# The first nine slots of an RWKV "wkv" kernel: set-up work, a state chain, zero matmuls and load order rearranged

## The chip, the cores and the metric

The kernel runs on one core of one Trainium2 chip. The metric is the device time of one execution in microseconds. A profiled execution also has a span, from its first instruction to its last, and the granted clock of TensorE.

## The reference

The inputs are k and v of 16 batches x 2048 steps x 256 channels in float32, and two rows w and u of 256. For each batch and channel a recurrence runs over time, kept in a scaled form (aa, bb, with the exponent pp):

```
for t in range(seq_len):
    kk, vv = k[b, t, :], v[b, t, :]
    ww = u + kk
    qq = max(pp, ww);  e1 = exp(pp - qq);  e2 = exp(ww - qq)
    output[b, t, :] = (e1 * aa + e2 * vv) / (e1 * bb + e2 + 1e-08)
    ww = pp - w + kk
    qq = max(ww, kk);  e1 = exp(ww - qq);  e2 = exp(kk - qq)
    aa = e1 * aa + e2 * vv;  bb = e1 * bb + e2;  pp = qq
```

So an output is a weighted mean of all earlier v, with weights that decay with w, plus the present one with its bonus u.

## The kernel before, in words

Time is cut into a head of T0 = 32 steps and 16 pieces ("steps" c = 0 to 15) of TC = 126, each of two halves of 63. A pair is one step with 4 of the 16 batches: time on the partitions, 4 x 256 channels along the free axis as two chunks of 512. Two pairs more (n = 2 and 3) hold the head for all batches. That makes 66 pairs; step 0 has the pairs 0, 1, 4 and 5.

The main loop (lines 636 to 693) has one slot n for each pair and 12 more. Its order is the order of the instructions on each engine, since the helper K pins every instruction behind the one issued before it on the same engine. In slot n:

- load(n + 6) issues the next loads; from pair 6 on k and v are both issued on POOL (lines 122 and 144). Each of k and v has six buffers. The first six k are issued on SP, the first v on POOL.
- exps(n) (ScalarE, lines 337 and 339) takes the exponential of X, two sets of logarithmic weights in PSUM, into the bf16 tile ez. Before pair 8 X is two tiles of two banks, each with an activation of its own; from pair 8 on it is one tile of four banks and one activation of 2048 columns, taken from a new pool (line 315).
- round_k(n + 1) (VectorE, line 307) copies the next k to float32r, and logs(n + 1) (TensorE, line 323) multiplies it by the matrices NLE and NLZ: four matmuls into X.
- times_v(n) (VectorE, line 346) multiplies half of ez by v; sums(n) (TensorE, line 377) adds rows of ez for the state.
- for a pair finished earlier: den (TensorE, line 525) and log_den (ScalarE, line 534) for q, invert (ScalarE, line 539) one slot later, and num (TensorE, line 547), mult (VectorE, line 555) and store two slots later. q is n - 10, for the head n - 6. So the head pairs have their den in slots 8 and 9, and pair 0 has it in slot 10.

Between steps a state is carried. The table PLANS places each part of it, as (slots after the last pair of the step, place in the slot, function): "a" places lie in ScalarE's order, "d" in VectorE's, "p" in TensorE's. small_work(n, place) issues what stands there. Within a slot the places come in the order a3, exps, d0, round_k, p0, num, d1, a0, p1, invert, a2, den and log_den, mult, d2, d3, a4, logs, num, p3, times_v and sums, p2, d4, mult and store, d5, p4, a1. For step 0 (plan "first", last pair 5) the parts are: copy_sums (ScalarE), turn_sums (TensorE), split_sums (VectorE, gives tsum), state_logs (ScalarE, gives lf), state_offset and state_near (VectorE), state_weights (ScalarE, w and g), state_sums, state_add and state_decay (VectorE, AB), inject_logs and inject_weights (ScalarE, y and phi), carry_weights and carries (VectorE, phi2 and ab), turn_carries (TensorE), and inject (line 495): VectorE copies the turned carries to row, and SP issues four DMAs of 8 KB that write them into rows 126 and 127 of the ez tiles of this step. den reads these two rows: for pair 0 the first two of the four DMAs must have landed. The plan "head" is a shorter chain for the pairs 2 and 3.

PSUM has eight banks: X four, psd (tag "den") two, psn (tag "num") one, pst (the sums) one. Until slot 66 den, turn_sums and turn_carries share the one psd tile, so each waits until the reader of the one before is done; psn holds the sums of the head until copy_sums, and num from slot 10 on.

Ahead of the loop stand the constant matrices. TensorE begins with 12 matmuls of zeros into psn (line 216). matrices_for_head (VectorE) stands at slot 0, place d1; the matrices that den and num need, matrices_for_outputs (It, Id, IdN), matrices_for_outputs_of_head (Lh, LhN) and more_matrices_for_outputs (Lf, LfN), stand at place d5 of slots 3, 4 and 5 (lines 627 to 629).

Of the kernel before, what the change touches and what calls it, by code (L numbers as in the profile page):

```python
# [7 lines left out]
F32 = mybir.dt.float32  # L8
# [14 lines left out]
def kernel(  # L23
# [32 lines left out]
    D = 2 * Dm  # L56
# [3 lines left out]
    AHEAD = 6  # L60
# [50 lines left out]
    def load(n):  # L111
        kr = kpool.tile([128, 4, Dm], F32, tag="kr", name="kr")
        vr = vpool.tile([128, 4, Dm], BF16, tag="vr", name="vr")
        kr_of[n], vr_of[n] = kr, vr
        c, p = pairs[n]
        if is_head(n):
            load_head(n, SP, kr, k)
        else:
            t0 = T0 + c * TC
            r = min(128, T - t0)  # L120

            K((SP if n < AHEAD else POOL).dma_start(  # L122
                out=kr[0:r, :, :], in_=k[4 * p:4 * p + 4, t0:t0 + r, :].rearrange("n t d -> t n d")))
            if n >= AHEAD:
                load_v(n)

    def load_head(n, eng, t, x):
# [25 lines left out]
    def row_of(a, b):  # L153
        return crow[a:b, :].unsqueeze(1).broadcast_to([b - a, 4, Dm])

    for n in range(AHEAD):
        load(n)
    K(SC.preload_act_table_set("natural_log_exp_and_others"))

# [49 lines left out]
        K(DVE.tensor_scalar(E[:, 0:N], E[:, 0:N], cw, None, ALU.add))  # L209


    zeros = consts.tile([128, D], BF16, tag="zeros", name="zeros")
    fill(zeros, 0.0)
    idle = psn.tile([128, D], F32, tag="num", name="idle")
    for i in range(12):
        K(PE.matmul(idle, zeros[:, 0:128], zeros, start=True, stop=True))

    for x in (kr_of, vr_of):
        fill(x[3][64:96, 0:2, :], 0.0)
# [371 lines left out]
    PLANS = {  # L591
        "head": ((1, "a0", copy_sums), (1, "p2", turn_sums), (2, "d1", split_sums), (2, "a1", state_logs),
                 (3, "a0", state_weights), (3, "d4", state_start)),
        "first": ((1, "a0", copy_sums), (1, "p3", turn_sums), (1, "d5", split_sums), (1, "a1", state_logs),
                  (2, "d1", state_offset, 0), (2, "d1", state_offset, 1), (2, "d1", state_near),
                  (2, "a0", state_weights), (2, "d3", state_sums), (2, "d3", state_add, 0),
                  (2, "d3", state_decay, 0), (2, "a1", inject_logs), (2, "a1", inject_weights),
                  (3, "d0", carry_weights), (3, "d0", carries), (3, "p0", turn_carries), (3, "d1", inject),
                  (3, "d4", state_add, 1), (3, "d5", state_decay, 1)),
        "steady": ((1, "a0", copy_sums), (1, "p2", turn_sums), (2, "d1", split_sums), (2, "a2", state_logs),  # L600
                   (2, "d3", state_offset, 0), (2, "d4", state_offset, 1), (2, "d5", state_near),
                   (3, "a0", state_weights), (3, "d2", state_sums), (3, "d3", state_add, 0),
# [33 lines left out]
    for n in range(NP + LAG + 2):  # L636
# [90 lines left out]
```

## Time and profile before

| what | value |
|---|---|
| median of 4 runs | 297.68 us (296.36 to 299.38) |
| the profiled execution | 298.33 us |
| its span | 296.6 us |
| its mean granted TensorE clock | 0.942 of full |
| ACT (ScalarE) busy | 264.9 us, 298 instructions |
| DVE (VectorE) busy | 252.9 us, 520 instructions |
| PE (TensorE) busy | 252.3 us, 1144 matmuls |
| POOL (GpSimd) busy | 162.1 us, most of it issuing DMAs |
| ACT busy in the first 45 us | 30.3 us |

All times of the trace are in microseconds from the start of the span. PEld is TensorE's weight load, which runs beside its matmuls; a name with q behind it (SPq) is the engine's sequencer, which issues DMAs. A line of a timeline gives start, length, engine, line of the kernel, operation, what it writes and reads (out<-in) with shapes, and in brackets the idle time of the engine ahead of it and what ended that. The row of digits gives the busy share, or the granted clock, of 40 equal slices in tenths.

### The profile page before, as it was taken

How to read it: one execution, taken by the hardware profiler on the slowest of the kernel's cores; microseconds unless marked ns; L12 is line 12 of the kernel's file. 1: busy time of each engine (PE TensorE's matmuls, PEld its weight loads, DVE VectorE, ACT ScalarE, POOL GpSimd, SP SyncE). 2: the span in 40 equal slices, each digit the busy share in tenths (PEclk: the TensorE clock that was granted, in tenths of full speed). 3: DMA queues.
4: the chain of work that ended last, by engine and by line, in shares of the span. 5: the costliest groups of instructions: out<-in, count | busy, mean ns of one | idle time of the engine just before them, and what ended most of it. 6: DMA issues, size and time to landing. Idle time of an engine off the chain costs nothing.

```text
span 296.6 us, 3976 instructions
## 1 busy us (share of the span) xinstructions
PE 252.3 (85%) x1144; PEld 115.8 (39%) x1144; DVE 252.9 (85%) x520; ACT 264.9 (89%) x298; POOL 162.1 (55%) x227
## 2 busy tenths in 40 slices
PE   8598688788999989889989898998989898788970
PEld 3245343344434434443434343444434443333430
DVE  5767668979998989999999999998999999778760
ACT  7665679789999999999999999999999999798990
POOL 8786346755665665565666555567655652212531
PEclk9855579999999999999999999999999999999995
DMA  6999999999999999999999999999999999245885
GB/s 184 249 275 303 302 254 203 257 293 290 296 322 333 333 330 332 330 335 342 333 331 327 330 324 329 337 342 336 320 335 321 325 311 271 89 146 189 281 269 183
DMA packets 59253, 85.94 MB, mean 290 GB/s; under 512 B 6834, under 2 KB 43430, under 8 KB 59232
## 3 DMA queue, kind: packets, MB, share of 16 engines
q0 software_dynamic: 52608, 81.73, 100.6%
q1 hardware_dynamic: 6592, 3.94, 5.0%
q8 instruction: 9, 0.15, 0.2%
q14 instruction: 12, 0.10, 0.1%
q10 hardware_dynamic: 32, 0.02, 0.0%
HBM read 68.12 MB, written 34.05 MB: 344 GB/s over the span
## 4 chain that ended last, share of the span: by engine, by line
ACT 29%; DVE 23%; PE 21%; issue 14%; DMA 11%; SPq 0%; POOL 0%; ACTq 0%; DVEq 0%; POOLq 0%
ACT ez L339 12%; ACT rd L534 8%; PE X L323 8%; DVE rd L555 7%; DVE ez L346 7%; ACT rd L539 5%; PE num L547 5%; PE den L525 4%; DMA kr<-in_k_dram 4%; DMA vr<-in_v_dram 4%; DVE km L307 3%; DMA out_dram<-rd 3%; PE tot L377 2%; PE den L395 2%; DVE ts L388 1%
## 5 line engine op out<-in xcount | busy, mean ns | idle before, releaser
L339 ACT ACTIVATE ez<-X 128x2048 bf16<-128x2048 f32 x58 | 109.3, 1885 | 6.1 <-PE num L547 3.9
L555 DVE TENSOR_TENSOR rd<-num,rd 128x512 f32<-128x512 f32 (+2 forms) x131 | 88.7, 685 | 8.6 <-ACT rd L539 4.3
L144 POOL DMA_DIRECT2D vr<-in_v_dram x64 | 54.7, 854 | 74.1 <-DVE ez L346 21.7
L346 DVE TENSOR_TENSOR ez<-ez,vr 126x2048 bf16<-126x2048 bf16 (+1 forms) x66 | 79.9, 1210 | 7.1 <-ACT ez L339 4.0
L575 POOL DMA_DIRECT2D out_dram<-rd x63 | 51.5, 818 | 48.8 <-issue 18.5
L534 ACT ACTIVATE rd<-den 128x1024 f32<-128x1024 f32 (+3 forms) x67 | 67.3, 1005 | 4.0 <-PE den L525 3.5
L539 ACT ACTIVATE rd<-rd 128x1024 f32<-128x1024 f32 (+3 forms) x67 | 70.3, 1049 | 0.3
L547 PE MATMUL num<-ez,LfN 128*128 128x512 bf16 x128 | 49.1, 384 | 10.0 <-DVE rd L555 9.9
L323 PE MATMUL X<-km,NLE 128*128 128x512 f32 x128 | 51.2, 483 | 7.4 <-ACT ez L339 2.5
L547 PE MATMUL num<-ez,IdN 126*128 126x512 bf16 (+1 forms) x131 | 49.8, 380 | 0.0
L307 DVE CAST km<-kr 126x1024 fp32r<-126x1024 f32 x64 | 47.8, 747 | 2.2 <-DMA kr<-in_k_dram 2.2
L122 POOL DMA_DIRECT2D kr<-in_k_dram x60 | 46.5, 774 | 2.9 <-issue 2.3
L323 PE MATMUL X<-km,NLZ 128*128 128x512 f32 x128 | 42.9, 418 | 0.0
L525 PE MATMUL den<-ez,Id 126*128 126x512 bf16 (+1 forms) x131 | 39.6, 382 | 0.0
L525 PE MATMUL den<-ez,Lf 128*128 128x512 bf16 x128 | 38.0, 378 | 1.8 <-DVE tsum L402 0.7
L323 PEld LDWEIGHTS X<-km,NLE 128*128 128x128 f32 x128 | 21.8, 200 | 25.6 <-ACT ez L339 14.7
L377 PE MATMUL tot<-ez,OHV 126*32 126x512 bf16 x128 | 26.5, 406 | 4.8 <-DVE ez L346 4.7
L323 PEld LDWEIGHTS X<-km,NLZ 128*128 128x128 f32 x128 | 25.7, 201 | 6.4 <-ACT ez L337 0.4
L377 PE MATMUL tot<-ez,OHE 128*32 128x512 bf16 x128 | 26.5, 411 | 0.0
L547 PEld LDWEIGHTS <-LfN 128*128 128x128 bf16 x128 | 12.3, 96 | 23.1 <-issue 20.5
L525 PEld LDWEIGHTS <-Lf 128*128 128x128 bf16 x128 | 12.4, 98 | 20.5 <-issue 8.6
L337 ACT ACTIVATE ez<-X 128x1024 bf16<-128x1024 f32 (+1 forms) x16 | 14.6, 966 | 5.6 <-PE X L323 5.5
(108 smaller groups left out, 195.9 us busy)
## 6 DMA issues: line engine op xcount, KB each, us to landing
out_dram<-rd POOLq DMA_DIRECT2D x60, 512.0 KB, 7.3
kr<-in_k_dram POOLq DMA_DIRECT2D x56, 512.0 KB, 8.3
vr<-in_v_dram POOLq DMA_DIRECT2D x60, 256.0 KB, 7.5
kr<-in_k_dram SPq DMA_DIRECT2D x4, 512.0 KB, 9.1
kr<-in_k_dram POOLq DMA_DIRECT2D x4, 504.0 KB, 8.8
ez<-row SPq DMA_DIRECT2D x64, 8.0 KB, 5.6
vr<-in_v_dram POOLq DMA_DIRECT2D x4, 252.0 KB, 8.1
out_dram<-rd POOLq DMA_DIRECT2D x2, 504.0 KB, 4.4
```

Source lines behind the costliest of these rows:

```text
L144: K(POOL.dma_start(out=vr_of[n][0:r, :, :], in_=v[4 * p:4 * p + 4, t0:t0 + r, :].rearrange("n t d -> t n d")))
L307: K(DVE.tensor_copy(KM[n][0:r, 0:i, :], kr_of.pop(n)[0:r, 0:i, :]))
L323: K(PE.matmul(X[q][:, i, :], m[0:kr, :], km[0:kr, i, :], start=True, stop=True))
L339: K(SC.activation(ez_of(n)[:, 0:4:2], X[2][:, :, 0:i, :], ACT.Exp))
L346: K(DVE.tensor_mul(ez[0:r, 1:4:2], ez[0:r, 0:4:2], vb[0:r].unsqueeze(1).broadcast_to([r, 2, i, D])))
L377: K(PE.matmul(TOT[c][y:y + 32], m[0:r, :], ez_of(n)[0:r, q, i, :], start=n == first_of[c], stop=n == last_of[c] or (head and i == 1), tile ...
L525: K(PE.matmul(d[:, i, :], m[0:r, :], ez_of(n)[0:r, q, i, :], start=q == 0, stop=q == 2, skip_group_check=True))
L534: K(SC.activation(RD[n][0:r, a:b, :], DEN[n][0:r, a:b, :], ACT.Ln, scale=RS))
L539: K(SC.activation(RD[n][0:r, a:b, :], RD[n][0:r, a:b, :], ACT.Exp, scale=-1.0))
L547: K(PE.matmul(d, m[0:r, :], ez_of(n)[0:r, q, i, :], start=q == 1, stop=q == 3, skip_group_check=True))
L555: K(DVE.tensor_mul(RD[n][0:r, i, :], NUM.pop((n, i))[0:r, :], RD[n][0:r, i, :]))
L575: K(eng.dma_start(out=out[4 * p + a:4 * p + b, t0:t0 + r, :].rearrange("n t d -> t n d"), in_=o[0:r, a:b, :]))
```

## The change

It makes five edits, all of them to the first nine slots.

1. Loads. k of pairs 0 and 1, and of the head, stay on SP; k of pairs 4 and 5 move from SP to POOL and are issued behind the v loads of pairs 2 and 3, each followed by its own v.
2. The 12 zero matmuls at the start write to psd instead of psn. In every slot from 0 to 8 two more follow logs(n + 1), and two more follow sums(n) (not in slot 4). Slots up to 4 (up to 3 behind the sums) use psd, the later ones psn.
3. The plan "head": state_logs moves from the end of slot 5 (a1) to slot 6, place a0, behind its exps.
4. The plan "first": state_logs moves from the end of slot 6 to slot 7, a0, behind the exps; state_offset and state_near from d1 to d3 of slot 7; state_weights to slot 8, a3, ahead of its exps; state_sums, state_add and state_decay to slot 8, d0; inject_logs and inject_weights to slot 8, a0, behind its exps; carry_weights and carries from d0 to d3 of slot 8; turn_carries from p0 to p3; inject from d1 to d4; state_add and state_decay of the second half to slot 9, d2 and d4.
5. The matrices for the outputs move to place d2 of slots 0, 1 and 2.

```
@@ load
-            K((SP if n < AHEAD else POOL).dma_start(
+            K((SP if n < 2 else POOL).dma_start(
                 out=kr[0:r, :, :], in_=k[4 * p:4 * p + 4, t0:t0 + r, :].rearrange("n t d -> t n d")))
-            if n >= AHEAD:
+            if n >= 2:
                 load_v(n)
...
-    for n in range(AHEAD):
+    for n in range(4):
         load(n)
...
-    idle = psn.tile([128, D], F32, tag="num", name="idle")
-    for i in range(12):
-        K(PE.matmul(idle, zeros[:, 0:128], zeros, start=True, stop=True))
+
+    def idle(pool, count):
+        t = pool.tile([128, D], F32, tag="num", name="idle") if pool is psn else pool.tile(
+            [128, 2, D], F32, tag="den", name="idle")[:, 0]
+        for i in range(count):
+            K(PE.matmul(t, zeros[:, 0:128], zeros, start=True, stop=True))
+
+    idle(psd, 12)
...
-    for n in range(2, AHEAD):
+    for n in range(2, 4):
         load_v(n)
+    for n in range(4, AHEAD):
+        load(n)
...
-        "head": (... (2, "a1", state_logs), ...
+        "head": (... (3, "a0", state_logs), ...
-        "first": ((1, "a0", copy_sums), (1, "p3", turn_sums), (1, "d5", split_sums), (1, "a1", state_logs),
-                  (2, "d1", state_offset, 0), (2, "d1", state_offset, 1), (2, "d1", state_near),
-                  (2, "a0", state_weights), (2, "d3", state_sums), (2, "d3", state_add, 0),
-                  (2, "d3", state_decay, 0), (2, "a1", inject_logs), (2, "a1", inject_weights),
-                  (3, "d0", carry_weights), (3, "d0", carries), (3, "p0", turn_carries), (3, "d1", inject),
-                  (3, "d4", state_add, 1), (3, "d5", state_decay, 1)),
+        "first": ((1, "a0", copy_sums), (1, "p3", turn_sums), (1, "d5", split_sums), (2, "a0", state_logs),
+                  (2, "d3", state_offset, 0), (2, "d3", state_offset, 1), (2, "d3", state_near),
+                  (3, "a3", state_weights), (3, "d0", state_sums), (3, "d0", state_add, 0),
+                  (3, "d0", state_decay, 0), (3, "a0", inject_logs), (3, "a0", inject_weights),
+                  (3, "d3", carry_weights), (3, "d3", carries), (3, "p3", turn_carries), (3, "d4", inject),
+                  (4, "d2", state_add, 1), (4, "d4", state_decay, 1)),
...
-    at(3, "d5", matrices_for_outputs)
-    at(4, "d5", matrices_for_outputs_of_head)
-    at(5, "d5", more_matrices_for_outputs)
+    at(0, "d2", matrices_for_outputs)
+    at(1, "d2", matrices_for_outputs_of_head)
+    at(2, "d2", more_matrices_for_outputs)
...
         if more:
             logs(n + 1)
+        if n < HALVES + 1:
+            idle(psd if n < 5 else psn, 2)
         if live and out_qp:
             num(qp, 1)
         small_work(n, "p3")
         if live:
             times_v(n)
             sums(n)
+        if n < HALVES + 1 and n != 4:
+            idle(psd if n < 4 else psn, 2)
         small_work(n, "p2")
```

More of the change, by code (lines that the diff above doesn't have):

```diff
@@ L591 @@
     PLANS = {
-        "head": ((1, "a0", copy_sums), (1, "p2", turn_sums), (2, "d1", split_sums), (2, "a1", state_logs),
+        "head": ((1, "a0", copy_sums), (1, "p2", turn_sums), (2, "d1", split_sums), (3, "a0", state_logs),
                  (3, "a0", state_weights), (3, "d4", state_start)),
-        "first": ((1, "a0", copy_sums), (1, "p3", turn_sums), (1, "d5", split_sums), (1, "a1", state_logs),
-                  (2, "d1", state_offset, 0), (2, "d1", state_offset, 1), (2, "d1", state_near),
-                  (2, "a0", state_weights), (2, "d3", state_sums), (2, "d3", state_add, 0),
-                  (2, "d3", state_decay, 0), (2, "a1", inject_logs), (2, "a1", inject_weights),
-                  (3, "d0", carry_weights), (3, "d0", carries), (3, "p0", turn_carries), (3, "d1", inject),
-                  (3, "d4", state_add, 1), (3, "d5", state_decay, 1)),
+        "first": ((1, "a0", copy_sums), (1, "p3", turn_sums), (1, "d5", split_sums), (2, "a0", state_logs),
[4 more added lines that the diff above has]
+                  (4, "d2", state_add, 1), (4, "d4", state_decay, 1)),
         "steady": ((1, "a0", copy_sums), (1, "p2", turn_sums), (2, "d1", split_sums), (2, "a2", state_logs),
```

## The prediction

> **What bounds the kernel now.** I read the page's busy shares first, then the stretches (busy time of each engine in chosen windows), then ScalarE's order of instructions in the first 50 us, then the instructions and DMAs around the first carry.
>
> ```profile
> PE 252.3 (85%) x1144; PEld 115.8 (39%) x1144; DVE 252.9 (85%) x520; ACT 264.9 (89%) x298; POOL 162.1 (55%) x227
> ...
> PEclk9855579999999999999999999999999999999995
> ```
> ```profile
> 100.00:150.00 50.00, 44.94 (x217) 20.62 (x216) 47.20 (x92) 48.82 (x53) 30.14 (x38) 1.00 1.17 331
> ```
>
> The columns of a stretch are its length, PE, weight loads, DVE, ACT and POOL busy, then the granted clock, the DMA share and GB/s. In the steady part ACT works 48.82 of 50 us: nothing that is lost early is caught up there, and what is won early is kept. The first 45 us are different: by the same view of 7.5 us each, ACT is busy 30.3 us in them, so 14.7 us are idle. The clock row says that TensorE had half its clock in about slices 2 to 5.
>
> ```profile
> 9.65:13.06 3.41, 1.38 (x7) 0.49 (x6) 2.62 (x12) 1.89 (x2) 2.29 (x4) 1.00 1.25 255
> 13.06:16.47 3.41, 3.41 (x11) 1.45 (x10) 2.19 (x3) 2.28 (x3) 2.47 (x4) 0.50 1.28 251
> ...
> 36.95:40.37 3.42, 3.42 (x12) 1.71 (x11) 1.99 (x4) 1.60 (x2) 1.80 (x3) 0.50 1.18 286
> 40.37:43.78 3.41, 2.58 (x13) 1.11 (x12) 2.08 (x3) 3.41 (x4) 0.56 (x1) 1.00 1.12 267
> ```
>
> I cut these stretches so that both clock changes (down at 13.06, up at 40.37) fall on a border. PE was 40% busy in the stretch before the fall, and 76% busy in one that kept the clock.
>
> ```profile
> 24.36 0.23 ACT L411 ACTIVATE S<-tsum 128x32 f32<-128x32 f32 x1 [0.84 <-DVE tsum L402]
> 24.99 1.94 ACT L337 ACTIVATE ez<-X 128x1024 bf16<-128x1024 f32 x2 [0.40 <-PE X L323]
> ...
> 30.59 0.26 ACT L414 ACTIVATE lf<-tsum 128x64 f32<-128x64 f32 x1 [3.06 <-DVE tsum L402]
> 30.76 1.92 ACT L337 ACTIVATE ez<-X 128x1024 bf16<-128x1024 f32 x2
> ...
> 34.84 1.88 ACT L339 ACTIVATE ez<-X 128x2048 bf16<-128x2048 f32 x1 [0.37 <-PE X L323]
> 38.09 1.02 ACT L534 ACTIVATE rd<-den 96x1024 f32<-96x1024 f32 x1 [1.37 <-PE den L525]
> 39.79 1.88 ACT L339 ACTIVATE ez<-X 128x2048 bf16<-128x2048 f32 x1 [0.69 <-PE X L323]
> ...
> 46.18 1.88 ACT L339 ACTIVATE ez<-X 128x2048 bf16<-128x2048 f32 x1
> ```
>
> These are start, length, instruction, and in brackets the idle time before it. The exps of slots 6, 7, 8, 9 and 11 start at 24.99, 30.76, 34.84, 39.79 and 46.18. The 3.06 us is state_logs of step 0, queued ahead of the exps of slot 7. From slot 11 on ACT hardly waits.
>
> ```profile
> 35.85 0.28 DVE L497 CAST row<-den 128x128 bf16<-128x128 f32 x1
> ...
> 36.22 26.61 SPq L501 DMA_DIRECT2D ez<-row  x8
> ...
> 36.75 1.23 DVE L346 TENSOR_TENSOR ez<-ez,vr 126x2048 bf16<-126x2048 bf16 x1 [0.61 <-ACT ez L339]
> ...
> 43.75 0.60 PE L525 MATMUL den<-ez,Lf 128*128 128x512 bf16 x2
> ```
> ```profile
> ez<-row SPq DMA_DIRECT2D x1, 8.0 KB, 5.4
> ```
> ```profile
> ez<-row SPq DMA_DIRECT2D x1, 8.0 KB, 6.7
> ```
>
> This is the first carry: row copied 1.0 us after the exps of slot 8 began and ahead of times_v(8), its DMAs issued from 36.22, den(0) at 43.75. The DMA rows are the last issue for step 0 (near 38.3) and the first for step 1 (near 59); between them others show 5.6 and 5.8.
>
> **The change, part by part.** I follow the path to exps(8), then to exps(11), and compare with the 34.84 and 46.18 of before.
>
> Matrices early. DVE sets slots 0 to 3. From 10.74, where the head matrices end, the chain in the new order is: outputs 0.81 (18.19 to 19.00), times_v(0) 1.22, km 0.68, head outputs 0.83 (22.15 to 22.98), times_v(1) 1.22, km 0.42, then Lf 1.33 (25.37 to 26.70), which ends near 17.1. That is 2.97 us of new work; 1.65 us of it falls into two waits for v (0.85 and 0.80 before times_v(1) and (2)) that were there anyway. times_v(2) now waits for exps(2), which end near 17.2 (km of slot 2 at 13.4; PE first does four zero matmuls and the sums, to about 14; first half of X at half clock 1.20). times_v(2) 1.22 and km 0.68 give 19.05; sums(2) and two zeros hold PE to 19.3, X takes 0.72 at full clock, and exps(4) start at 20.05 instead of 19.04: 1.0 us lost. Without the cover of the v waits it would be up to 2.7.
>
> Loads. k4 and k5 leave SP's queue (issued 5.4 and 5.9) and stand on POOL behind the v of slots 2 and 3, issued at about 10.4 and 12; each costs POOL 0.77 and pushes k6 back by up to 1.5. k loads issued on POOL at 13.9 to 19.5 took 7.2 to 10.2 us, so k4 lands at 17.6 to 20.6; it is needed at 18.4. Cost 0 to 2.2 us. I take 0, since the nearest row (13.93) is the 7.2 one. The v loads get nothing: DVE is late for them now.
>
> Zero matmuls: 34 in slots 0 to 8, each 0.43 us at half clock (12 took 5.20) and about 0.22 at full clock (an estimate: the two den matmuls at 43.75 take 0.60 together and 0.38 each, so they start 0.22 apart). They buy the clock. At full clock X takes 0.72 for its first half and 1.28 for four (48.89 to 50.17), instead of 1.20 and 2.26; turn_sums 0.62 instead of 1.05. In the slots where PE waits they cost nothing; after sums they stand ahead of the next X, 0.43 a slot.
>
> State chain. Slot 4: exps 20.05 to 22.0, copy_sums 0.5, exps(5) at 22.6. times_v(4) 1.22 to 23.25, sums and turn_sums to 24.7, X 0.72: exps(6) at 25.4 (24.99 before; the 0.84 wait goes, but X was the later of the two). They end at 27.35; S, g and ts take 1.0; exps(7) at 28.35 (30.76 before: the 3.06 wait is gone). X(7), two zeros and turn_sums end at 29.7, split 0.36, km(8) 0.69, X(8) 1.28: exps(8) at 32.2 instead of 34.84. So 2.6 us are won up to here, and what is late next is split_sums ahead of km(8) on DVE.
>
> The carry. All of this chain now lies behind exps(8): 1.88 + y and phi 0.70 (33.77 to 34.47) + carry weights and carries 0.54 (34.79 to 35.33) + times_v(8) 1.22, which stands ahead of the copy, + row 0.28 = 4.7 us after exps(8), where it was 1.3. The second DMA of the first group is issued 0.6 later and takes 5.8 (ends 5.4 and 6.7): landed at exps(8) + 11.1 = 43.3, where 43.75 stood before. The path without it: 1.88 + 0.70 + 1.02 (log_den 2) + 1.88 + 1.05 + 0.58 + 1.88 (exps 10), about 0.1 less at each seam, would let log_den(0) start at exps(8) + 9.2 = 41.4. PE has nothing past num(2,0), from about 39.8 to 43.3; den(0) is next in its queue, and X(11) is behind den(0). So den(0) at 43.3, 1.04 long at full clock, X(11) 1.28, exps(11) at 45.7: only 0.5 of the 2.6 us is left.
>
> The clock in that pause. 3.5 us without a matmul is more than any stretch of before had; the 40% stretch was followed by half clock. At half clock den(0) takes 1.86 (36.19 to 38.05) and X(11) 2.26, 1.8 us more: exps(11) at 47.5, 1.3 after. The fall may come up to a stretch later, so the value lies between -0.5 and +1.3, plus 0.6 for a second such stretch; I take +0.9, near the full price, as almost any cut of 3.41 us puts half of the pause in one stretch. ACT has no slack afterwards, so +0.9 goes to the end.
>
> Sum: +1.0 (to slot 4) - 3.6 (slots 5 to 8) + 2.1 (carry) + 1.4 (clock) = +0.9. The profiled execution is 298.33 us (span 296.6), 0.65 above the median of 297.68; it becomes 299.2, the median 298.6.
>
> Two rules to weigh. The Trainium skill, "DMA: Bandwidth & Descriptors", section "Anatomy of one DMA", puts a DMA at about 2.0 us plus bytes over 436 GB/s. An estimate by that page is 2.0 us for the 8 KB rows; the carry would be there before it is needed and the sum would be -2.6 us. The rows with 5.4 to 6.7 under a DMA share near 1.2 decide against it. "TensorE: Matmul & The Clock Gate", Part 1, says that about 3.4 us of sustained activity lifts the clock; by that rule the stretch from 13.06, 3.41 of 3.41 us busy, would have lifted it, and it stayed at 0.50, so the zeros' purchase is not sure either.
>
> **The rivals.** (A) The carry is late but the clock holds, as in the stretch with 76%: exps(11) at 45.7, so -0.5 and a median of 297.2. Against it: the pause is longer than any shown. (B) The carry is no longer last, because its DMAs land in under 4 us or PE's first slots run quicker: -2.6 to -3.9 (exps(11) at 42.3), median 294.3. For it: the shortest of all 64 such DMAs took 2.1 us; against it: between 36 and 60 us the shortest took 5.4. (C) Slower: the zeros do not lift the clock. A slot then costs PE 2.05 (X) + 0.61 (sums) + 1.73 (zeros) = 4.4 us against 2.7, with 5.3 us of pauses between 9.65 and 33.5 to swallow them. Four such slots cost 6.9 less half of the pauses, 4.3 us: median 302.0; it decides when the clock is still half at slot 4. Against it: the stretch from 36.95, full of 512-column matmuls, did lift it.
>
> **How the numbers follow.** Main case 0.56, its own range 297.2 to 300.4; A 0.18, B 0.14, C 0.12. The range 294.2 to 301.0 leaves out half of B and most of C. Over 1% (2.98 us, about what a measurement can tell): faster, most of B and a trace of A, 0.13; slower, C and the upper end of the main case, 0.17; within 1%, 0.70.
>
> **What would show it.** Right: ACT's wait for tsum before lf gone; exps(8) near 32; row copied after times_v(8); den(0) held by the DMA of the carry with PE idle some 3 us; a clock of 0.5 in a stretch near 44. Wrong: exps(8) later than 33.5; no PE wait at den(0); half clock throughout slots 2 to 7; km(4) waiting for k4.

## The result, and the profile after

The changed kernel takes 296.79 us (median of 43 runs, 294.69 to 302.93) against 298.35 us of the kernel before (62 runs, 295.87 to 301.39). The ratio is 0.9949, with a 95% interval from 0.9933 to 0.9964: half a per cent faster, 1.5 us, where the forecast said 0.9 us slower. The profiled execution took 296.52 us with a span of 294.8 us (before 298.33 and 296.6), at a mean granted clock of 0.986 (before 0.942). Ratios leave disturbed runs out and belong each to the runs of the kernel before on the same chip, whose median went from 297.26 to 298.63, so a ratio need not be the quotient of two medians.

First the page of the changed kernel, the same two rows that were shown of before:

```profile
PE 251.5 (85%) x1178; PEld 114.2 (39%) x1178; DVE 252.7 (86%) x520; ACT 264.9 (90%) x298; POOL 164.4 (56%) x229
...
PEclk9999979999999999999999999999999999999996
```

ACT's work is the same 264.9 us; PE has 34 matmuls more and is 0.8 us less busy, because the long stretch at half clock (the 5s of before) is gone: the first half of X(4) takes 0.70 us where it took 1.19. One dent is left, the 7 in the sixth slice (37 to 44 us).

ScalarE's order of instructions after (start, length, and in brackets the idle time ahead and what ended it):

```profile
18.50 1.94 ACT L344 ACTIVATE ez<-X 128x1024 bf16<-128x1024 f32 x2 [1.75 <-PE X L330]
...
27.93 0.27 ACT L421 ACTIVATE lf<-tsum 128x64 f32<-128x64 f32 x1
...
29.40 1.88 ACT L346 ACTIVATE ez<-X 128x2048 bf16<-128x2048 f32 x1
...
42.90 1.02 ACT L541 ACTIVATE rd<-den 128x1024 f32<-128x1024 f32 x1 [4.46 <-PE den L532]
44.41 1.88 ACT L346 ACTIVATE ez<-X 128x2048 bf16<-128x2048 f32 x1 [0.48 <-PE X L330]
```

These are exps(4), lf, exps(8), log_den(0) and exps(11). Exps(4) of before, which the forecast gave only as a number:

```profile
19.04 1.94 ACT L337 ACTIVATE ez<-X 128x1024 bf16<-128x1024 f32 x2 [1.83 <-PE X L323]
```

The 3.06 us ahead of lf are gone, exps(8) start 5.44 us earlier than before; then ACT stands still for 4.46 us at log_den(0), and exps(11) are only 1.77 us early. The span is 1.8 us shorter: what is left at exps(11) is carried to the end unchanged.

The carry on DVE, in SP's queue and on PE, and the stretches around it (length, PE, weight loads, DVE, ACT, POOL busy, clock, DMA share, GB/s):

```profile
32.37 1.22 DVE L353 TENSOR_TENSOR ez<-ez,vr 126x2048 bf16<-126x2048 bf16 x1
33.50 0.28 DVE L504 CAST row<-den 128x128 bf16<-128x128 f32 x1
```
```profile
33.87 0.55 SPq L508
34.46 6.41 DMA ez<-row
41.00 1.86 PE den L532 x4
```
```profile
41.00 1.01 PE L532 MATMUL den<-ez,Lf 128*128 128x512 bf16 x2 [4.02 <-DMA ez<-row]
```
```profile
37.19:40.60 3.41, 0.00 (x0) 0.00 (x0) 1.96 (x3) 1.26 (x2) 1.56 (x3) 1.00 1.23 309
40.60:44.01 3.41, 3.01 (x8) 1.75 (x8) 0.00 (x0) 1.02 (x1) 0.00 (x0) 0.50 1.24 295
```

The row is copied 4.1 us after exps(8) start, behind times_v(8); the chain (second fence) has its DMA in flight for 6.41 us; den(0) waits 4.02 us for it; no matmul runs in the stretch before 40.60, and half clock follows for one stretch.

All profiles in one table. "To slot 4" is the start of exps(4); the next two columns are the steps from exps(4) to exps(8) and on to exps(11); then the median and its ratio.

| kernel | to slot 4 | 4 to 8 | 8 to 11 | exps(11) | median us | ratio (95%) |
|---|---|---|---|---|---|---|
| before | 19.04 | 15.80 | 11.34 | 46.18 | 298.35 | 1 |
| after | 18.50 | 10.90 | 15.01 | 44.41 | 296.79 | 0.9949 (0.9933 to 0.9964) |
| e1_no_zeros | 19.13 | 11.17 | 14.67 | 44.97 | 298.78 | 1.0047 (1.0016 to 1.0078) |
| e2_matrices_late | 17.99 | 12.33 | 13.42 | 43.74 | 298.14 | 1.0010 (0.9978 to 1.0041) |
| e3_chain_before | 18.90 | 12.88 | 11.09 | 42.87 | 295.64 | 0.9927 (0.9895 to 0.9959) |
| e4_loads_before | 19.57 | 10.91 | 12.84 | 43.32 | 297.85 | 0.9978 (0.9951 to 1.0005) |
| e5_no_carry_wait | 18.66 | 10.90 | 9.83 | 39.39 | 293.14 | 0.9805 (0.9766 to 0.9844) |
| e6_clock_kept | 19.23 | 10.90 | 13.14 | 43.27 | 295.69 | 0.9888 (0.9848 to 0.9928) |
| e7_chain_early | 18.58 | 12.37 | 14.02 | 44.97 | 297.57 | 0.9969 (0.9932 to 1.0006) |
| e8_chain_early_psn | 20.52 | 12.24 | 13.26 | 46.02 | 297.08 | 0.9948 (0.9917 to 0.9978) |
| e9_before_chain_filled | 19.00 | 12.64 | 10.57 | 42.21 | 294.94 | 0.9934 (0.9911 to 0.9957) |
| e10_filled_psn | 18.84 | 12.65 | 11.20 | 42.69 | 295.17 | 0.9932 (0.9917 to 0.9947) |
| e11_row_first_filled | 19.42 | 10.90 | 13.68 | 44.00 | 296.33 | 0.9978 (0.9959 to 0.9998) |
| e12_chain_early_filled | 20.93 | 12.50 | 10.57 | 44.00 | 295.19 | 0.9920 (0.9900 to 0.9941) |
| f1_after_again | 19.53 | 10.90 | 13.80 | 44.23 | 297.00 | 1.0000 (0.9965 to 1.0035) |
| f2_clock_kept_again | 21.24 | 10.91 | 13.08 | 45.23 | 295.51 | 0.9933 (0.9907 to 0.9960) |
| f3_loads_held | 19.54 | 10.90 | 12.55 | 42.99 | 296.52 | 0.9973 (0.9944 to 1.0002) |
| f4_loads_held_clock_kept | 19.37 | 10.91 | 13.07 | 43.35 | 295.67 | 0.9929 (0.9905 to 0.9952) |

Two things are to be read from it ahead of the experiments. The step from slot 4 to slot 8 is 10.90 or 10.91 in all eight profiles that leave the zeros, the matrices and the chain as the change has them up to slot 8, and in e11; it is a property of the order of work. The start of slot 4 is not: in the fourteen profiles whose first slots are those of the changed kernel it lies between 18.50 and 21.24, in the middle 19.3. A single profile's exps(8) therefore can't price an edit to within 1 us, but the step of 4 to 8 can.

### The profile page after: what moved, and what is told of

Its sections match the earlier page's. It is cut to its first block, busy times and chain, and to the rows that moved or that the text cites. A ratio compares the mean times of both kernels' runs of the same rounds, so it can differ in the third digit from the quotient of the medians.

```text
span 294.8 us, 4044 instructions
## 1 busy us (share of the span) xinstructions
PE 251.5 (85%) x1178; PEld 114.2 (39%) x1178; DVE 252.7 (86%) x520; ACT 264.9 (90%) x298; POOL 164.4 (56%) x229
## 4 chain that ended last, share of the span: by engine, by line
ACT 26%; DVE 24%; PE 19%; DMA 14%; issue 13%; SPq 1%; POOL 0%; ACTq 0%; DVEq 0%
ACT ez L346 11%; DVE ez L353 7%; ACT rd L541 7%; DVE rd L562 7%; DMA vr<-in_v_dram 5%; PE X L330 5%; PE num L554 5%; PE den L532 4%; ACT rd L546 4%; DMA kr<-in_k_dram 4%; DMA out_dram<-rd 3%; DVE km L314 2%; DMA ez<-row 2%; DVE ts L395 2%; PE den L402 2%
## 5 line engine op out<-in xcount | busy, mean ns | idle before, releaser
L143 POOL DMA_DIRECT2D vr<-in_v_dram x64 | 53.9, 842 | 63.5 <-DVE ez L353 19.4
L582 POOL DMA_DIRECT2D out_dram<-rd x63 | 53.0, 842 | 49.5 <-issue 18.5
L330 PE MATMUL X<-km,NLE 128*128 128x512 f32 x128 | 48.9, 463 | 3.0 <-ACT ez L346 1.7
L121 POOL DMA_DIRECT2D kr<-in_k_dram x62 | 48.3, 778 | 3.6 <-DMA kr<-in_k_dram 3.2
L330 PE MATMUL X<-km,NLZ 128*128 128x512 f32 x128 | 40.7, 399 | 0.2 <-ACT ez L344 0.2
L384 PE MATMUL tot<-ez,OHV 126*32 126x512 bf16 x128 | 25.2, 385 | 4.4 <-DVE ez L353 4.3
L330 PEld LDWEIGHTS X<-km,NLE 128*128 128x128 f32 x128 | 20.9, 191 | 19.8 <-ACT ez L346 13.0
L330 PEld LDWEIGHTS X<-km,NLZ 128*128 128x128 f32 x128 | 24.2, 190 | 6.4 <-ACT ez L344 0.9
L384 PE MATMUL tot<-ez,OHE 128*32 128x512 bf16 x128 | 25.2, 390 | 0.0
```

What stands on the lines that cost most here:

```text
L143: K(POOL.dma_start(out=vr_of[n][0:r, :, :], in_=v[4 * p:4 * p + 4, t0:t0 + r, :].rearrange("n t d -> t n d")))
L330: K(PE.matmul(X[q][:, i, :], m[0:kr, :], km[0:kr, i, :], start=True, stop=True))
L384: K(PE.matmul(TOT[c][y:y + 32], m[0:r, :], ez_of(n)[0:r, q, i, :], start=n == first_of[c], stop=n == last_of[c] or (head and i == 1), tile ...
L582: K(eng.dma_start(out=out[4 * p + a:4 * p + b, t0:t0 + r, :].rearrange("n t d -> t n d"), in_=o[0:r, a:b, :]))
```

## The experiments

### One part undone at a time

The theory: the first slots gave more than forecast, and the late carry with its half clock took back most. The rival: the carry cost nothing that matters, and the gain was simply smaller.

**The zeros out** (e1). Both calls of idle in the loop are removed.

```
-        if n < HALVES + 1:
-            idle(psd if n < 5 else psn, 2)
...
-        if n < HALVES + 1 and n != 4:
-            idle(psd if n < 4 else psn, 2)
```

> The changed kernel without the 34 zero matmuls in slots 0 to 8; the 12 at the start stay. Theory (the zeros keep the clock up and so win most of the early slots): the clock falls in the first 15 us and stays at half until about 37; exps(8) start at 31.5 to 32.5 instead of 29.40; since the carry hangs on exps(8), exps(11) moves by nearly the same amount: 2 to 3 us later, ratio to before 1.002 to 1.008. Rival (the zeros stand in the way: the chain that ended last runs through 2.0 us of them in slots 3 and 4, and the clock does not need them): exps(8) at 28.5 or earlier, ratio 0.990 to 0.993.

Measured: 298.78 us, ratio 1.0047 where the changed kernel has 0.9949. The zeros are worth about 1%. The stretches of e1:

```profile
12.73:16.14 3.41, 3.41 (x10) 1.72 (x10) 3.10 (x13) 1.99 (x3) 3.41 (x6) 0.50 1.11 257
...
36.62:40.03 3.41, 1.31 (x8) 0.31 (x6) 3.38 (x6) 2.78 (x4) 1.50 (x2) 1.00 1.26 299
...
43.44:46.86 3.42, 3.42 (x13) 1.51 (x11) 1.00 (x2) 2.74 (x3) 0.00 (x0) 0.50 1.25 300
46.86:50.27 3.41, 3.41 (x11) 1.85 (x11) 2.58 (x6) 1.47 (x3) 2.42 (x4) 0.50 0.86 168
```

Half clock from 12.73 to 22.97 and again from 40.03 to 50.27, three stretches each. In slots 4 to 8 it costs only 0.27 us (11.17 against 10.90); most is lost behind exps(11), where ACT has no slack: the span runs on for 252.4 us from exps(11), that of the changed kernel for 250.4. The ratio came as the theory had it; exps(8) did not (30.30, where 31.5 to 32.5 was expected), because the clock rose again at 22.97 and not at 37. One half-clock stretch lowers a run's mean clock by 3.41 x 0.5 / 295 = 0.0058. The twelve runs of e1 have 0.948 to 0.969 (middle 0.959), the twelve of f1, the changed kernel again, 0.971 to 0.992 (middle 0.982): about four stretches more, and no run of e1 reaches the lowest of f1. So what the zeros buy is the clock.

**The matrices back in slots 3 to 5** (e2).

```
-    at(0, "d2", matrices_for_outputs)
-    at(1, "d2", matrices_for_outputs_of_head)
-    at(2, "d2", more_matrices_for_outputs)
+    at(3, "d5", matrices_for_outputs)
+    at(4, "d5", matrices_for_outputs_of_head)
+    at(5, "d5", more_matrices_for_outputs)
```

> The changed kernel with the matrices for the outputs back at the end of slots 3, 4 and 5. Theory (they cost up to 1 us in slots 0 to 2, where the chain runs through DVE, and win it back in slots 3 to 5): exps(4) start 0.5 to 1 us before 18.50, exps(8) within 0.7 us of 29.40, ratio to before 0.993 to 0.998. Rival (moving them is where the time is won): exps(8) 1.3 us or more later, ratio 0.999 or above.

Measured: ratio 1.0010, so the early matrices are worth about 0.6%. The step from 4 to 8 grows from 10.90 to 12.33; slot 4 starts at 17.99, some 1.3 us ahead of the middle of the others. The ratio is on the rival's side, exps(8) at 30.32 lie between the two. The change thus moves DVE's work out of slots 3 to 5, where it shows in the step, and pays for a part of it in slots 0 to 2, as the forecast had it; the ratios say that more is won than paid, the two profile columns alone (+1.43 and -1.3) do not. The profiled run of e2 (296.10 us) is one of its two fastest, so where the runs near the median of 298.14 lose their time is in no profile.

**The state chain as before** (e3): the plan "first" is that of before (the lines with a minus in the diff of the change), all other edits stay.

```
-        "first": (... (2, "a0", state_logs), ...
+        "first": (... (1, "a1", state_logs), ...
```

> The changed kernel with the plan "first" put back to what it was; the other edits stay. Theory (the landing of the first carry sets slot 10, so what the slots before win is given back): the exps of slot 8 start later than in the changed kernel, at about 31.6 instead of 29.40, because state_logs again waits for tsum ahead of the exps of slot 7, but row is copied about 1 us after they start and not 4; PE's wait for the carry at den(0) falls from 4.0 us to under 1, and exps(11) start at about 42, 2.5 us before the 44.41 of the changed kernel: ratio to before about 0.985 to 0.988. Rival (the new plan is what wins the time, and half clock is what loses it): exps(11) later than 44.41 by up to the 3.06 us wait that comes back, ratio 0.997 to 1.005.

Measured: 295.64 us, ratio 0.9927, about half the gain that the theory had: no worse than the changed kernel, with an interval that overlaps. ScalarE, and two stretches:

```profile
28.01 0.26 ACT L421 ACTIVATE lf<-tsum 128x64 f32<-128x64 f32 x1 [1.30 <-DVE tsum L409]
...
31.78 1.86 ACT L346 ACTIVATE ez<-X 128x2048 bf16<-128x2048 f32 x1
35.55 1.03 ACT L541 ACTIVATE rd<-den 96x1024 f32<-96x1024 f32 x1 [1.91 <-PE den L532]
...
42.87 1.88 ACT L346 ACTIVATE ez<-X 128x2048 bf16<-128x2048 f32 x1
```
```profile
27.79:31.20 3.41, 1.72 (x11) 0.81 (x8) 2.08 (x9) 2.42 (x6) 1.50 (x2) 1.00 1.26 287
31.20:34.62 3.42, 3.04 (x11) 0.87 (x11) 2.67 (x6) 2.35 (x3) 1.83 (x2) 0.50 1.28 295
```

The old chain keeps ACT waiting 1.30 us before lf, and exps(8) come 1.98 us later in the step (12.88); but its carry is in time, the step to exps(11) is 11.09 instead of 15.01, and exps(11) start at 42.87, 1.54 us ahead of the changed kernel. In these profiles the new chain gives away at the carry more than it wins before it.

**The loads as before** (e4).

```
-            K((SP if n < 2 else POOL).dma_start(
+            K((SP if n < AHEAD else POOL).dma_start(
...
-            if n >= 2:
+            if n >= AHEAD:
...
-    for n in range(4):
+    for n in range(AHEAD):
```

> The changed kernel with the loads issued as before (k of pairs 4 and 5 on SP ahead of all v of pairs 2 to 5). Theory (the later k leave the DMA engines to the first k and v, so k1 lands 0.5 us sooner and DVE waits for no v): exps(4) 0.6 to 1.5 us later than 18.50, with waits for v at times_v(1) and (2) back in part; ratio to before 0.997 to 1.001. Rival (the loads do nothing, since DVE is late for v anyway): exps(4) within 0.3 us of 18.50, ratio 0.994 to 0.996.

Measured: ratio 0.9978, interval 0.9951 to 1.0005, 0.3% from the changed kernel and inside the scatter of both. The step from 4 to 8 is the same. Exps(4) at 19.57 and the ratio came as the theory had them, but 19.57 is inside the scatter of that column, and the profile has two stretches of half clock (42.20 to 49.03), most of them behind exps(11). Whether the loads are worth anything stays open.

The prices do not add up. Undone alone, the zeros are worth 1.0% and the matrices 0.6%, while the whole change is worth 0.5%; the chain's 0.2% of loss and the loads' 0.3% of gain are inside the intervals. What one part wins depends on the others.

### The price of the carry and of the clock

**The carry not waited for** (e5) and **the clock kept** (e6). In e5 den and num of step 0's four pairs read 126 rows instead of 128, which leaves the head's carried state out of step 0's outputs. In e6 sixteen zero matmuls stand ahead of den(0).

```
-        rl, ri = (NH, NH) if is_head(n) else (128, TC)
+        rl, ri = (NH, NH) if is_head(n) else (TC if pairs[n][0] == 0 else 128, TC)
```
```
+                if n == LAG:
+                    idle(psd, 16)
```

> The changed kernel, but den and num of the four pairs of step 0 read 126 rows of ez and not 128: this leaves the state carried out of the head out of the outputs of step 0, and with it the wait of den(0) for the carry's DMAs; the DMAs themselves are still issued. Theory (the landing of the carry sets slot 10 and brings the half clock after it): no PE wait at den(0), log_den(0) at about 38.4 instead of 42.90, exps(11) at about 39.4 instead of 44.41, no half clock near 41; 4 to 5 us less than the changed kernel, ratio to before 0.977 to 0.983. Rival (slots 9 to 11 are held by something else as well, such as DVE or the banks of X, so that the wait covers other work): exps(11) at 42 or later, ratio 0.988 or above.

> The changed kernel with 16 more zero matmuls (3.5 us at full clock) into the den tile ahead of den(0), in the pause in which PE waits for the carry. Theory (the clock falls because PE pauses 4.0 us, and this costs about 1.3 us): the wait for the carry stays but is filled, the clock stays full, den(0) takes 1.05 instead of 1.86 us and X(11) 1.3 instead of 2.1; exps(11) at about 43.0 to 43.4 instead of 44.41 where the carry lands at the same time; ratio to before 0.988 to 0.992. Rival (the clock has no part in it, only the landing): exps(11) within 0.4 us of 44.41, or later because the zeros stand ahead of den(0); ratio 0.994 to 0.997.

Measured: 293.14 us (ratio 0.9805) and 295.69 us (0.9888). ScalarE of e5, then PE and one stretch of e6:

```profile
29.56 1.88 ACT L346 ACTIVATE ez<-X 128x2048 bf16<-128x2048 f32 x1
...
38.48 1.02 ACT L541 ACTIVATE rd<-den 128x1024 f32<-128x1024 f32 x1
39.39 1.88 ACT L346 ACTIVATE ez<-X 128x2048 bf16<-128x2048 f32 x1
```
```profile
37.61 3.62 PE L219 MATMUL idle<-zeros 128*128 128x512 bf16 x15
41.28 0.59 PE L532 MATMUL den<-ez,Lf 128*128 128x512 bf16 x2
...
41.96 0.82 PE L330 MATMUL X<-km,NLE 128*128 128x512 f32 x2
```
```profile
41.00:45.00 4.00, 3.94 (x22) 1.98 (x20) 1.28 (x3) 2.66 (x2) 0.01 (x1) 1.00 1.28 291
```

Without the carry log_den(0) waits for nothing (the bracket is gone) and slots 8 to 11 take 9.83 us. With the carry but at full clock they take 13.14: den(0) 0.59 instead of 1.01, X(11) 0.82 instead of 1.41 for its first half. Between these two, on the same chip and both with full clock in their profiles, the carry costs 2.55 us in the medians (295.69 against 293.14) and 3.31 in the step from 8 to 11, of which e5 loses about 1 us again behind exps(11) (its span runs on for 251.8 us from there, that of e6 for 250.7). In e6 den(0) follows the zeros with no wait for the DMA in brackets, so some tenths of this may be the zeros' own; f3 below, with the carry waited for at full clock and no zeros, takes 12.55 us, 2.7 more than e5. The expected mechanism is shown by this: the carry is last, and waiting for it costs about 2.5 us.

**The clock alone, repeated** (f1, f2): the changed kernel and e6, twelve runs each on one chip.

> The changed kernel itself, beside the next three. Theory (the half clock after the pause costs 1 to 2 us and its length differs from run to run): median 1 to 2 us above f2_clock_kept_again, with a spread of 2 us or more between its runs. Rival (the difference between e6_clock_kept and the changed kernel was one of chips): within 0.5 us of it.

> The changed kernel with 16 zero matmuls in the pause ahead of den(0), as in e6_clock_kept. Theory: 1 to 2 us below f1_after_again and a spread under 1.5 us. Rival: within 0.5 us of f1_after_again.

Measured: 297.00 us (295.01 to 301.13) and 295.51 us (294.98 to 297.51): with the clock kept behind the pause the median is 1.5 us lower (1.3 without the 301.13 of f1) and the spread 2.5 us instead of 6.1, more than the 1.5 us expected. The runs of f1 sort by their mean clock: 295.01 us at 0.992, 296.15 to 297.17 at 0.985 to 0.987, 298.54 to 301.13 at 0.971 to 0.979, with a single one (296.64 at 0.980) between. The runs of f2 all have 0.985 or more. The profile of f1 shows the fall that the forecast had seen coming for slot 2, and that the profile of the changed kernel had not:

```profile
9.91:13.32 3.41, 1.68 (x10) 0.50 (x9) 3.16 (x14) 1.39 (x2) 2.64 (x5) 1.00 1.24 203
13.32:16.74 3.42, 3.42 (x12) 1.45 (x12) 3.16 (x13) 1.94 (x2) 3.42 (x5) 0.50 1.19 304
```
```profile
9.65:13.06 3.41, 2.10 (x12) 0.77 (x11) 3.10 (x15) 1.33 (x2) 3.04 (x6) 1.00 1.33 213
```

The first fence is f1, the second the changed kernel: with 1.68 us of PE work in the stretch the clock fell, with 2.10 it held (2.10 as well in the changed kernel's own stretch, 9.86 to 13.27). That is the same kernel twice; which case a run gets depends on where the 3.41 us stretches lie and on when the loads land. f2's profile shows the latter: v of pair 0 came late, and everything with it, so that slot 4 started at 21.24.

```profile
12.82 1.22 DVE L353 TENSOR_TENSOR ez<-ez,vr 126x2048 bf16<-126x2048 bf16 x1 [1.41 <-DMA vr<-in_v_dram]
```

That f1's ratio is 1.0000 while that of all 43 runs is 0.9949 fits: five of its twelve runs were in the group with the lowest clock.

### Can the carry be early and the state chain too?

**The chain one slot earlier** (e7), and with the turned carries in the num bank (e8).

```
-                  (3, "a3", state_weights), (3, "d0", state_sums), ...
-                  (3, "d3", carry_weights), (3, "d3", carries), (3, "p3", turn_carries), (3, "d4", inject),
+                  (2, "a4", state_weights), (2, "a4", state_sums), ...
+                  (2, "a4", carry_weights), (2, "a4", carries), (2, "p3", turn_carries), (2, "p3", inject),
```

> The changed kernel with the first state chain run through in slot 7: state_weights to inject_weights on ScalarE ahead of the exps of slot 8, carries and the copy of row ahead of times_v(7). Theory: the exps of slot 8 start about 1.3 us later (30.7 instead of 29.40), row is copied at about 31.7 instead of 33.5, the carry lands near 38.8, and the wait at den(0) falls below 1 us; exps(11) at 41 to 42 instead of 44.41, no half clock after it; ratio to before 0.983 to 0.988. Rival (what the chain wins at the carry it takes on ScalarE and on the bank that den(2) shares with the turned carries): exps(11) at 43.5 or later, ratio 0.992 or above.

> As e7_chain_early, with the turned carries of step 0 in the PSUM bank of num, which stands free until slot 10, so that den(2) need not wait for the copy of row. Theory: log_den(2) starts 0.3 to 1 us earlier than in e7_chain_early and the slots 8 to 10 with it; ratio to before 0.981 to 0.987. Rival (the shared bank is not what ends last): within 0.001 of e7_chain_early.

Measured: ratios 0.9969 and 0.9948, so the expectation that an early carry pays fell, and the rival's wait came. PE of e7:

```profile
31.68 0.23 PE L499 MATMUL den<-It,ab 128*128 128x128 bf16 x1 [1.71 <-DVE ab L493]
...
33.42 0.61 PE L384 MATMUL tot<-ez,OHV 126*32 126x512 bf16 x2 [1.19 <-DVE ez L353]
...
34.79 1.06 PE L532 MATMUL den<-ez,Lh 96*128 96x512 bf16 x2
```

The carry is issued in time, but PE waits 1.71 us for DVE's chain and 1.19 us for times_v(7), now behind it; den(2) slips to 34.79, ACT waits 3.94 us at log_den(2), and the clock falls as well (half from 32.85 to 39.67). The wait for the carry at den(0) has become a wait at den(2). Freeing the den bank (e8) leaves 3.61 us of it, so the bank was at most 0.3 us of it.

**Zeros ahead of logs(8) to keep the clock**: with the old chain (e9), with the old chain and the num bank (e10), with the chain early (e12); and with the new chain but the row copied ahead of times_v(8) (e11, which keeps the 16 zeros of e6 and leaves out those of slot 8). The edit common to e9 and e10:

```
+        if n == HALVES - 1:
+            idle(psn, 7)
```

> e3_chain_before (the changed kernel with the plan "first" of before) plus seven zero matmuls ahead of logs(8), in the 1.70 us in which PE there waits for the exps of slot 7. Theory (a pause of PE over about half of a 3.4 us stretch costs a stretch at half clock, and the carry is no longer last in this order): the clock stays full through slots 7 to 11, den(2) ends about 1 us earlier, exps(11) start at 41.5 to 42.2 instead of 42.87; ratio to before 0.983 to 0.988, and the runs lie within 2 us of each other. Rival (the clock after slot 8 is not what holds e3_chain_before): exps(11) within 0.4 us of 42.87, ratio 0.991 to 0.994.

> As e9_before_chain_filled, with the turned carries of step 0 in the bank of num, so that den(2) does not wait for the copy of row. Theory: log_den(2) 0.3 to 0.7 us earlier than in e9, ratio 0.001 to 0.002 below it. Rival (exps(9) wait for X(9), not for den(2)): no difference beyond 0.001.

> The changed kernel with its new plan, the 16 zero matmuls in the pause at den(0) as in e6_clock_kept, and the carry brought forward inside slot 8: turned in the bank of num, no zeros ahead of it, row copied ahead of times_v(8) instead of behind. Theory (the landing of the carry sets slot 10, one for one): row copied at exps(8) + 3.6 instead of + 4.1, den(0) and exps(11) 0.5 us earlier than in e6_clock_kept relative to exps(8), ratio 0.985 to 0.988. Rival (times_v(8) behind row delays X(10) by more than this): ratio 0.989 or above.

> e7_chain_early with its two faults mended: times_v(7) ahead of the carries on VectorE, the turned carries in the bank of num, and six more zeros in PE's pause of slot 7. Theory: log_den(2) waits under 1.5 us instead of 3.94, full clock throughout, den(0) not held by the carry for more than 1 us; exps(11) at 41 to 42; ratio 0.982 to 0.987. Rival (what stands on ScalarE ahead of the exps of slot 8 costs as much as the carry wins): ratio as e6_clock_kept, 0.988 to 0.991.

Measured: 294.94, 295.17, 296.33 and 295.19 us. PE of e9 at the carry:

```profile
40.21 0.59 PE L532 MATMUL den<-ez,Lf 128*128 128x512 bf16 x2 [0.52 <-DMA ez<-row]
```

The carry is late by 0.52 us where it was late by 4.02, den(0) takes 0.59 at full clock, and exps(11) start at 42.21, 2.2 us ahead of the changed kernel and 0.66 ahead of e3. Its ratio, 0.9934, is nevertheless where the rival had it and not at 0.983 to 0.988. e10 shortened ACT's wait at log_den(2) from 1.13 to 0.80 and got 1.08 at log_den(0) instead: no difference in time, as its rival had it. e11 fell: the row was copied 0.6 us earlier (exps(8) + 3.53 instead of + 4.10 in e6), but times_v(8) and with it X(10) went later, and exps(10) stand at exps(8) + 7.34 instead of + 6.72 in e6. Its den(0), at 42.00, follows the sixteen zeros with no wait for the DMA, so what an earlier row wins by itself is not shown. e12 shows the early chain at 10.57 for slots 8 to 11, but pays 1.6 us for it in slots 4 to 8 and is no quicker than e9; its 0.9920 is above both of the ranges that were expected. The intervals of e3, e6, e9, e10, e12, f2 and f4 all overlap; they are 0.7 to 1.1% faster than before; e9 has the lowest median of those that compute everything, and is 1.9 us below the changed kernel in the medians; the ratios, which take out the difference between chips, leave 0.15% with overlapping intervals. f1 and f2, on the same chip, are the clean pair: 297.00 against 295.51 us between the changed kernel and one with its clock kept.

### Why the rows take so long to land

**Loads held back** (f3, and f4 with the clock kept): the loads of pairs 13 to 15 are issued at the end of slot 9 instead of in slots 7 to 9.

```
-        if n + AHEAD < NP:
+        if n + AHEAD < NP and n not in (7, 8, 9):
...
+        if n == 9:
+            for m in (13, 14, 15):
+                load(m)
```

> The changed kernel with the loads of pairs 13, 14 and 15 issued at the end of slot 9 instead of at the start of slots 7, 8 and 9, so that the DMA engines run dry while the carry is on its way. Theory (the 6.4 us from issue to landing are mostly queueing behind loads): the rows land 3 us or less after their issue, the wait at den(0) falls from 4.0 to about 1 us, and exps(11) start at about 42 instead of 44.41, if k13 is there in time; ratio 0.985 to 0.991. Rival (the latency is that of the DMA itself): the wait at den(0) stays at 3.5 us or more, and the late loads make it slower than the changed kernel: ratio 0.995 to 1.003.

> f3_loads_held with the 16 zero matmuls in the pause. Theory: where the carry lands early the zeros (3.5 us) stand in the way of den(0) by up to 1.5 us, so this is no better than f3_loads_held, within 0.5 us of it either way. Rival (the carry lands as late as before): as f2_clock_kept_again, or slower.

Den(0) of f3, the two stretches of f3 in which the rows are in flight, and that of f1:

```profile
41.00 0.59 PE L532 MATMUL den<-ez,Lf 128*128 128x512 bf16 x2 [2.93 <-DMA ez<-row]
```
```profile
36.28:39.69 3.41, 1.79 (x10) 0.62 (x8) 3.38 (x6) 3.25 (x4) 1.70 (x3) 1.00 1.28 283
39.69:43.10 3.41, 2.10 (x10) 1.19 (x10) 0.58 (x1) 1.04 (x2) 0.74 (x1) 1.00 1.27 300
```
```profile
37.22:40.63 3.41, 0.78 (x6) 0.13 (x3) 2.95 (x4) 2.25 (x2) 1.62 (x3) 1.00 1.26 313
```

The wait at den(0) is 2.93 us, between the theory and the rival; the ratio, 0.9973, is where the rival had it. In the chain that ended last the row DMA is in flight for 5.36 us, against 6.41 in the changed kernel and 5.01 in f1, which has no such edit. The DMA share is 1.28 and 1.27, no lower than in f1: what was issued earlier was still moving, so the load on the DMA engines was not lowered and the experiment can't tell whether it is the cause. The times are those of the kernels without the edit (f3 296.52 against f1 297.00, f4 295.67 against f2 295.51). Why 8 KB take 5 us and more stays open.

The stretches show something else. In f3 a border, at 39.69, cuts the pause of 2.93 us in two; both stretches keep enough work (1.79 and 2.10 us), and the clock holds with no zeros at all. In f1 the pause is shorter, 2.64 us, but lies in one stretch, which is left with 0.78 us, and the clock falls. So f3's good profile (295.29 us) is luck, not its edit.

## Why the prediction was wrong

The mechanism was told rightly, point by point: lf waits no more; the row is copied behind times_v(8); den(0) is held by the carry's DMA with PE idle (forecast some 3 us, measured 4.02 and, in f1, 2.64); half clock follows near 44 (40.60 to 44.01); nothing is caught up afterwards; and the loads, put at 0, held nothing up (km(4) waits for no k4). One sign was missed: exps(8) came at 29.40, not near 32. Of the rivals, none came as told: the clock did not hold (A), the carry was not hidden (B), the zeros did lift the clock (C); of B the half "PE's first slots run quicker" was true.

What failed is the first half of the sum, "+1.0 (to slot 4) - 3.6 (slots 5 to 8)". By step, forecast and the two profiles of the changed kernel against the profile of before:

| step | forecast | profile | f1 |
|---|---|---|---|
| to slot 4 | +1.0 | -0.54 | +0.49 |
| slots 5 to 8 | -3.6 | -4.90 | -4.90 |
| carry and clock, to exps(11) | +3.5 | +3.67 | +2.46 |
| sum | +0.9 | -1.77 | -1.95 |

Slots 5 to 8 were mis-sized by 1.3 us, and this is the part that repeats. The largest part is slot 7. There the forecast laid X(7), two zeros and turn_sums end to end from the end of exps(6) on, so that turn_sums ended 1.35 us after exps(7) began, and split_sums, km(8) and X(8) hung behind it. In the profile X(7) begins 0.24 us before exps(6) end, the matmuls overlap, and turn_sums ends 0.82 us after exps(7) begin. PE, ACT, DVE and PE after:

```profile
24.98 0.70 PE L330 MATMUL X<-km,NLE 128*128 128x512 f32 x2
...
26.28 0.66 PE L402 MATMUL den<-Ir,ts 128*128 128x48 f32 x4
```
```profile
26.12 1.93 ACT L344 ACTIVATE ez<-X 128x1024 bf16<-128x1024 f32 x2
```
```profile
26.98 0.36 DVE L409 COPY tsum<-den 128x192 f32<-128x192 f32 x1 [0.36 <-PE den L402]
27.25 0.68 DVE L314 CAST km<-kr 126x1024 fp32r<-126x1024 f32 x1
```
```profile
28.11 0.73 PE L330 MATMUL X<-km,NLE 128*128 128x512 f32 x2 [0.30 <-ACT ez L344]
```

Split_sums and km(8), said to be "late next" ahead of X(8), end at 27.93, before exps(7) do; X(8) waits for exps(7) to free its bank instead, and the slot takes 3.28 us where 3.85 was forecast. Slots 4 to 6 were each 0.1 to 0.3 too long (2.30, 2.48 and 2.84 instead of 2.55, 2.8 and 2.95) for a like reason: lengths were laid end to end where the rows overlap. On ACT ts starts at 20.32 and exps(4) end at 20.44; on PE sums, turn_sums and the first half of X(6) take 1.56 us from the end of times_v(4), where the forecast had 2.15. Undoing one part at a time divides the 4.90: the chain 1.98 (e3), the matrices 1.43 (e2), the zeros 0.27 (e1), the loads 0 (e4), together 3.7; the other 1.2 comes only with all of them, and what it consists of was not tried.

The term to slot 4 was set by a fall of the clock at 13.06 taken over from the profile of before. In the profile of the changed kernel the fall did not come (2.10 us of PE work in that stretch); in f1 it came, and slot 4 still began 0.5 us sooner than forecast: times_v(2) starts there at 16.56, directly behind Lf, where the forecast let it wait for exps(2) until 17.2. Over the fourteen profiles the term is about +0.3 (19.3 against 19.04) with a scatter from -0.5 to +2.2, so +1.0 was too high, but within what one profile can show.

The third term came near: 3.5 forecast, 3.67 and 2.46 measured. With the clock kept the step from 8 to 11 is 13.14 (e6) and 13.08 (f2) against the 11.34 of before, so the carry is +1.8 and +1.7 where 2.1 was forecast. The half clock adds 1.87 in the profile (15.01 against 13.14), 0.72 in f1 (13.80 against 13.08) and 1.5 in the medians of f1 and f2, where 1.4 was forecast. One side sum does not come out: the terms of the path without the carry add up to 9.0, and to less with 0.1 off at each seam, not to 9.2, and invert(3), 0.63, is missing from them; e5 has 8.92, and no term hung on it. With the first terms at the +0.3 and -4.9 of the profiles in the place of +1.0 and -3.6, the sum would have been -1.1 and had the right sign.

The Trainium skill, "TensorE: Matmul & The Clock Gate", section "HAM oscillation", gives the rule that PE should have no idle gap above about 3.4 us. The length of the stretch agrees (3.41 us between clock changes here), the rule does not go far enough: in e3 the longest gap was 1.70 us, and the clock fell after a stretch with 1.72 us of work. The same skill's "DMA: Bandwidth & Descriptors", section "Anatomy of one DMA", fits its 2.0 us plus bytes over 436 GB/s to DMAs issued from GpSimd. The rows are issued from SP, so the forecast's estimate of 2.0 us went beyond the section; 6.41 us were measured in the changed kernel, 5.36 in f3 and 5.01 in f1.

## What to carry to other kernels

Before adding up a chain over several engines, mark at each step which engine is the later one: where the bound engine does small work of its own, the others run ahead, and their steps cost nothing. Take a step from start to start in a row of the same clock; lengths laid end to end made four slots 1.3 us too long here. When a wait is removed by moving work later, follow what hangs on the end of that work: here 2.0 us of waiting were won in slots 4 to 8 and more than that was lost at a DMA that nobody had been waiting for. Where a pause of TensorE can't be avoided, a few matmuls of zeros in it keep the clock, and the runs lie closer together (f2 against f1). They cost little as long as they end before what TensorE waits for.

## What was not expected of the hardware

- The clock's fall follows from the work in one stretch of 3.41 us, not from one long gap: it fell after 0.00, 0.78, 1.31, 1.38, 1.68 and 1.72 us of PE work (changed kernel, f1, e1, before, f1, e3) and held after 1.79, 2.10 and 2.58 (f3, changed kernel, before). Counted in stretches of 3.41 us from the first rise of the clock to the end of all 18 profiles, every one of the 31 full-clock stretches with 1.72 us or less was followed by half clock, and none of the more than 1400 with 1.79 us or more. So the border lies between 1.72 and 1.79 in these runs, about half of the stretch.
- A full stretch does not always lift it. In e1 two stretches with 3.41 and 3.42 us of PE work stayed at 0.50 (12.73 and 43.44), in f1 one with zeros among its matmuls was followed by full clock at once. Half clock lasted 3.41, 6.83 or 10.24 us in the experiments. What decides on the length was not found. A hint: with the small matmuls of the sums (tot and turn_sums) left out of the count, the 11 half-clock stretches with under 2.24 us of PE work were followed by half clock and the 7 with 2.93 us or more by full clock, while the 8 between went both ways.
- The clock goes with much of the spread of a kernel's runs, but not with all of it. In f1 the five slowest runs (298.54 to 301.13 us) have the five lowest clocks, and with zeros in the pause (f2) the spread is 2.5 us instead of 6.1. But e2 has 296.10 and 298.89 us at 0.985 and 0.986, and e10 stays within 0.4 us at clocks from 0.981 to 0.990.
